# A two-layer decoder step: the odd layer's in-projection and both output projections by seven block products in place of eight, with the sums of weight blocks formed beside the even layer

## The chip, the cores and the metric

The kernel runs on one core of one Trainium2 chip, as one program. The metric is device time in microseconds of that core. The kernel before took 2334.9 us (median of three runs, 2333.31 to 2335.68).

## What is computed

One inference step over a prompt of 2048 tokens and 32 sample rows (8 sequences of 4 tokens), with D = 1024. Each layer normalises its input, projects it, mixes along the tokens, and projects back onto the residual. Cut to the lines that matter here:

```python
def even_mixer(h, w_in, b_fox, lb, hgrn_gain, w_out, hgrn_s0, fox_attend):
    proj = h @ w_in                                       # 1024 -> 4100 columns
    ...                                                   # HGRN2 recurrence on 4 heads, forgetting attention on 4
    out = jnp.concatenate([o_a, o_b], axis=-1) @ w_out    # 1024 -> 1024
def odd_mixer(h, w_in, w_gate, b_gate, gla_gain, w_out, gla_s0):
    proj = h @ w_in                                       # 1024 -> 3088 columns
    q, k, v, g, r = _split(proj, [512, 512, 1024, 1024, 16])
    log_f = jax.nn.log_sigmoid(r @ w_gate + b_gate) / 16
    ...                                                   # gated linear attention on 4 heads, dv = 256
    return o @ w_out, s                                   # 1024 -> 1024
def run_trunk(x, ...):
    for l in range(2):
        x = x + mixer(rmsnorm(x, norm[l]))
    return rmsnorm(x, final_norm), ...
```

## The kernel before, in words

**Products.** Every value that enters a product is scaled by a power of two and kept as two float16 parts, `hi` and `lo`. A product is three matmuls on TensorE (`mm3`): hi x hi, hi x lo, lo x hi. Over 1024 inputs (`KT` = 8 blocks of 128) that makes 24 matmuls for an output tile. They accumulate in a PSUM bank (512 float32 a partition), which VectorE or ScalarE then drains.

```python
    def mm3(self, ps, lh, rh, first, last):
        nc.tensor.matmul(ps, lh[0], rh[0], start=first, stop=False)
        nc.tensor.matmul(ps, lh[0], rh[1], start=False, stop=False)
        return nc.tensor.matmul(ps, lh[1], rh[0], start=False, stop=last)
```

**Units.** A weight unit is 256 columns (272 with the 16 gate columns). `half_unit` gives its four steps: fetch, measure (maximum), scale, and split into hi and lo. The tokens go in two halves of 1024; the 32 samples ride with the first. `proj_tm` puts tokens on the partitions (tiles of 128 tokens x 256 columns, two to a bank), `proj_fm` puts columns there (128 columns x 352 or 512 tokens, banks tagged `pj`, three of them). `few_rows` does the samples as strips of 32 rows, four side by side.

**Stages.** `phase_even` does the even in-projection in two halves of 16 units; the HGRN2 recurrence of a head (`lin_attn`) runs beside the next units. `phase_fox` does attention. `phase_odd` does the even output projection (2 halves x 4 units), the odd in-projection (2 halves x 12 units: for each head values `Cv`, query and key `Cqk`, gate `Cg`) with the recurrences beside it, and the odd output projection (2 halves x 4 units).

**Beside the second even half** `later_unit` reads each of the 20 later weight units once and takes its maximum and scale. The odd stage then fetches each unit again, once for each half, and splits it there.

**Activations.** `y_pieces` splits the mixer's output (`yT`, in memory) into hi and lo for the output projection. Between the layers `norm_store` normalises a tile of 128 rows and writes its hi and lo to `xs` in memory, and `norm_fetch` reads them back transposed, 17 transfers of 512 KB.

**Order.** A generator yields the cost of what it has just issued; `mux` interleaves two of them in proportion. A scheduler then places each instruction in its engine's queue by its own estimate of the times, and each engine takes its queue in order. Weight fetches, stores and transposes are issued by SyncE's queue (SP).

```python
            def recur(hf, h, a):
                return mux(lins[hf](h), LIN_O[hf], dense(a, a + 3), 66000.0)
```

Of the kernel before, what the change touches and what calls it, by code (L numbers as in the profile page):

```python
# [1 line left out]

# [17 lines left out]
P = 128  # L20
D = 1024
# [20 lines left out]
EY = 3  # L42
OY = 2
VPOOL = 1
XO = ("kt", "y", "vp", "c4", "sg")
TAG1 = "o"
PRT = ("st", "o")
# [15 lines left out]
YPOOL = (2, 6)  # L63
# [62 lines left out]
class Kern:  # L126
    def __init__(self, ctx, tc, ins, outs):
        self.ctx, self.tc, self.nc = ctx, tc, tc.nc
        self.i, self.o = ins, outs
        self.loaded, self.bank, self.n_xo = {}, 0, 0  # L130


    def consts(self):
# [30 lines left out]
        self.xs = dp.tile([NTOK, 2 * D], F16, name="xs")  # L164

    def more_consts(self, mp):
# [63 lines left out]
        for g in range(3):  # L230
            m = self.rowmask[g * TS : (g + 1) * TS]
            nc.gpsimd.affine_select(m, m, [[-DS, DB]], ALU.is_ge, 0.0, base=0, channel_multiplier=1)
            nc.gpsimd.affine_select(m, m, [[DS, DB]], ALU.is_ge, 0.0, base=DS - 1, channel_multiplier=-1)

# [87 lines left out]
    def half_unit(self, pool, pps, w, cols, key, nm, undo=None, k=1.0, also=(), raw=("wr", WU), scaler=None):  # L322
# [7 lines left out]
        def fetch():  # L330
            t["raw"] = pool.tile([P, KT, raw[1]], F32, tag=raw[0], name=f"wr_{nm}")
            for a, off, n, src in self.sources(w, cols, h):
                with nc.allow_non_contiguous_dma(reason="a few columns"):
                    nc.sync.dma_start(t["raw"][:, a * h : (a + 1) * h, off : off + n], src)
# [29 lines left out]

    def later_unit(self, pool, pps, w, cols, key, undo=None):

        nc = self.nc
        h, width, t = KT // WSPLIT, sum(n for _, n in cols), {}

        def fetch():  # L370
            t["raw"] = [pool.tile([P, h, WU], F32, tag="lr", name=f"lr_{key}{a}") for a in range(WSPLIT)]
            for a, off, n, src in self.sources(w, cols, h):
                with nc.allow_non_contiguous_dma(reason="a few columns"):
                    nc.sync.dma_start(t["raw"][a][:, :, off : off + n], src)

        def parts():
            t["m"] = pool.tile([P, WSPLIT + 1], F32, tag="rm", name=f"rm_{key}")
            return [r[:, :, :width] for r in t["raw"]]

        return (fetch,) + self.unit_scale(key, parts, lambda: t["m"], pool, pps, key, undo, 1.0)  # L380
# [145 lines left out]
    def norm_store(self, pool, hf, tiles, gain, lead):  # L526
# [3 lines left out]
        todo = self.few_first(self.ttiles(hf))  # L530
        fly = {}

        def load(x):
            c0, n = todo[x]
            fly[x] = [y[:n] for y in tiles(c0)]
            dc = T if c0 >= HALF else hf * HALF + c0
            with ExitStack() as st:
                if self.last_turn is not None:
                    st.enter_context(self.tc.issue_after(self.last_turn.ins))
# [1661 lines left out]
```

## Time and profile before

| What | us |
|---|---|
| median of the runs | 2334.9 |
| span of the profiled execution | 2333.0 |
| even layer, first half | 0 to 478 |
| even layer, second half | 478 to 862 |
| attention | 862 to 1283 |
| even output projection | 1283 to 1452 |
| odd layer, first half | 1452 to 1843 |
| odd layer, second half | 1843 to 2155 |
| odd output projection | 2155 to 2333 |

The borders are where the dense units of a stage begin in the trace; recurrences reach a little over them. In the views a row of a window gives its borders, its length, the busy time of each engine with the number of instructions, then the clock that was granted to TensorE (1.00 is full), the share of the DMA engines and the bandwidth. PE is TensorE's matmuls, PEld its weight loads (which overlap them), DVE VectorE, ACT ScalarE, POOL GpSimd. Matmuls overlap in the records, so that the busy time of one is longer than its share of the pace. A row of the timeline gives start, duration, engine, line, operation and operands (out<-in), and in brackets the idle time ahead of it with what ended it.

### The profile page before, as it was taken

What the parts mean: (1) busy time and instruction counts of PE and PEld (TensorE: products, weight loads), DVE (VectorE), ACT (ScalarE), POOL (GpSimd) and SP (SyncE); (2) the same over time, 40 slices, a digit from 0 to 9 for tenths busy, and PEclk for the clock granted to TensorE, in tenths of its full rate; (3) what the DMA queues carried; (4) which work ended last, traced back from release to release, by engine and by line L of the source; (5) the groups of instructions that cost most, each with busy time, mean ns of one, the idle gap of its engine ahead of it and who ended that gap; (6) DMA issues with size and microseconds to landing.
All of it is one profiled execution on the core that took longest, in us unless ns stands there. A gap on an engine that the chain in (4) does not pass through costs nothing. (4 is left out here: it accounts for less than half of the span.)

```text
span 2333.0 us, 58124 instructions
## 1 busy us (share of the span) xinstructions
PE 2251.4 (96%) x23060; PEld 1603.5 (69%) x23060; DVE 1447.7 (62%) x3313; ACT 1075.0 (46%) x2360; POOL 767.3 (33%) x818
## 2 busy tenths in 40 slices
PE   7999999999999999999999999999999999999998
PEld 5677667864655875665445888677677666666887
DVE  7766568537655757666767445366775655547554
ACT  6434344333332325555656543546545545545343
POOL 2333324112212214223335445144552422322232
PEclk9999999999999999999999999999999999999999
DMA  7232335765441268776982968523233431115553
GB/s 201 66 90 68 96 107 157 179 169 139 145 138 40 90 171 280 230 246 196 275 256 96 337 200 255 147 84 118 75 114 87 122 107 58 46 59 163 161 195 150
DMA packets 375665, 344.87 MB, mean 148 GB/s; under 512 B 107633, under 2 KB 322994, under 8 KB 375394
## 3 DMA queue, kind: packets, MB, share of 16 engines
q1 hardware_dynamic: 373250, 334.54, 48.2%
q0 software_dynamic: 2144, 6.62, 0.8%
q8 instruction: 181, 2.97, 0.5%
q14 instruction: 90, 0.74, 0.1%
HBM read 244.54 MB, written 79.63 MB: 139 GB/s over the span
## 5 line engine op out<-in xcount | busy, mean ns | idle before, releaser
L607 PE MATMUL pt_o<-w_o,act 128*128 128x256 f16 x1024 | 278.7, 273 | 1.8 <-POOL act L1790 1.8
L605 PE MATMUL pt_o<-w_o,act 128*128 128x256 f16 x1024 | 278.9, 273 | 0.6 <-ACT sg1C L662 0.6
L606 PE MATMUL pt_o<-w_o,act 128*128 128x256 f16 x1024 | 278.9, 273 | 0.0
L605 PEld LDWEIGHTS <-act 128*128 128x128 f16 x2304 | 226.6, 98 | 38.0 <-issue 4.0
L607 PEld LDWEIGHTS <-act 128*128 128x128 f16 x2304 | 226.7, 98 | 32.3 <-POOL act L1790 2.2
L606 PEld LDWEIGHTS <-act 128*128 128x128 f16 x2304 | 226.6, 98 | 30.7 <-issue 1.9
L605 PE MATMUL pt_Cv<-w_Cv,act 128*128 128x256 f16 (+1 forms) x512 | 140.9, 275 | 0.1
L606 PE MATMUL pt_Cv<-w_Cv,act 128*128 128x256 f16 (+1 forms) x512 | 141.0, 275 | 0.0
L607 PE MATMUL pt_Cv<-w_Cv,act 128*128 128x256 f16 (+1 forms) x512 | 140.9, 275 | 0.0
L772 POOL TENSOR_TENSOR kA<-kA,fA 128x512 f32<-128x512 f32 (+1 forms) x56 | 78.0, 1392 | 188.6 <-PE gl_A L738 142.5
L772 POOL TENSOR_TENSOR kC<-kC,fC 128x512 f32<-128x512 f32 (+1 forms) x56 | 83.6, 1492 | 153.4 <-PE gl_C L738 101.7
L1407 POOL TENSOR_SCALAR L<-L,nm 128x512 f32<-128x512 f32 (+3 forms) x160 | 99.3, 635 | 98.2 <-DVE nm L1403 42.3
L1399 ACT ACTIVATE L<-L,nm,kc 128x512 f32<-128x512 f32 (+3 forms) x160 | 118.3, 741 | 24.7 <-DVE nm L1397 23.8
L1434 ACT ACTIVATE th<-pt 128x512 f16<-128x512 f32 (+3 forms) x159 | 81.8, 528 | 90.2 <-PE pt L1427 87.0
L1435 DVE TENSOR_TENSOR tl<-pt,th 128x512 f16<-128x512 f32 (+3 forms) x159 | 95.2, 609 | 20.5 <-ACT th L1434 18.6
L1427 PE MATMUL pt<-ident,L 128*128 128x128 f32 x544 | 90.3, 278 | 1.4 <-POOL L L1407 1.0
L1551 PEld LDWEIGHTS pkt<-ident,pgcache_fox_k 128*128 128x128 f32 x512 | 58.4, 141 | 43.3 <-issue 25.1
L1889 ACT ACTIVATE vC<-pt_Cv,kc 128x512 f32<-128x512 f32 (+1 forms) x40 | 23.9, 598 | 129.8 <-PE pt_Cv L607 129.8
L1427 PEld LDWEIGHTS pt<-ident,L 128*128 128x128 f32 x544 | 66.5, 143 | 24.6 <-DVE tl L1435 4.8
L1551 PE MATMUL pkt<-ident,pgcache_fox_k 128*128 128x128 f32 x512 | 77.6, 278 | 5.5 <-DVE kts L1556 1.6
L1374 POOL TENSOR_TENSOR cm<-cb,caus 128x128 f32<-128x128 f32 x64 | 29.0, 454 | 135.7 <-DVE mx L1391 114.5
L605 PE MATMUL pt_Bk<-w_Bk,act 128*128 128x256 f16 x256 | 71.4, 279 | 2.3 <-DVE Bvs L1049 2.3
(959 smaller groups left out, 6752.9 us busy)
## 6 DMA issues: line engine op xcount, KB each, us to landing
pgcache_fox_k<-in_cache_fox_k SPq DMA_DIRECT2D x128, 256.0 KB, 4.2
pgcache_fox_v<-in_cache_fox_v SPq DMA_DIRECT2D x128, 256.0 KB, 4.1
yr<-yT SPq DMA_DIRECT2D x16, 1024.0 KB, 7.9
x1d<-xo SPq DMA_DIRECT2D x44, 256.0 KB, 4.2
wr_Aqf<-in_w_in_even SPq DMA_DIRECT2D x64, 128.0 KB, 3.3
wr_o<-in_w_out_even SPq DMA_DIRECT2D x32, 256.0 KB, 5.2
xo<-in_x_prompt SPq DMA_DIRECT2D x32, 256.0 KB, 5.2
wr_Cv<-in_w_in_odd SPq DMA_DIRECT2D x32, 256.0 KB, 4.0
```

The costliest lines, as they stand in the source:

```text
L605: nc.tensor.matmul(ps, lh[0], rh[0], start=first, stop=False)
L606: nc.tensor.matmul(ps, lh[0], rh[1], start=False, stop=False)
L607: return nc.tensor.matmul(ps, lh[1], rh[0], start=False, stop=last)
L772: nc.gpsimd.tensor_tensor(kv[:, :, 0], kv[:, :, 0], t1.to_broadcast([P, nb, w]), ALU.mult)
L1374: self.last_cm = nc.gpsimd.tensor_tensor(cm, cb[:, tb * P : (tb + 1) * P], caus, ALU.add)
L1399: self.last_exp = nc.scalar.activation(lt[:, :w], lt[:, :w], AF.Exp, bias=nm[:, 0:1], scale=ib, accum_out=nm[:, 2 + j : 3 + j])
L1407: nc.gpsimd.tensor_scalar(lt[:, :w], lt[:, :w], nm[:, 1:2], 2.0**14, ALU.mult, ALU.mult)
L1427: nc.tensor.transpose(pt[:, w : w + P], rows[b][s // 4][0][:, (s % 4) * P : (s % 4 + 1) * P], self.ident)
L1434: nc.scalar.activation(th[:, a:w], pt[:, a:w], AF.Copy),
L1435: nc.vector.tensor_tensor(tl[:, a:w], pt[:, a:w], th[:, a:w], ALU.subtract)))
L1551: last = nc.tensor.transpose(pk[:, j * P : (j + 1) * P], pgs[j][:, h * P : (h + 1) * P], self.ident)
L1889: r = nc.scalar.activation(v[h][:, g : g + cnt], ps[:, :, :256], AF.Copy, scale=c)
```

## The change

With the tokens of a half (or of a piece) as two row blocks, the 1024 inputs as two column blocks, and the columns of a unit as two blocks, a product of 2 x 2 blocks takes eight block products. The change takes seven (one level of the Strassen-Winograd form). The seven left operands are A11, S1, S2, S4, S3, A12, A22, where S are sums and differences of blocks of activations, and the right ones B11, T1, T2, B22, T3, B21, T4 of weights. The output's sums are made by accumulation: three banks, x, z and y, take the products in the order x z x z x y x, and a bank is drained after each product, with add, into the output block that needs it at that point.

```diff
+SEVEN = (("x", "A11", "B11"), ("z", "S1", "T1"), ("x", "S2", "T2"), ("z", "S4", "B22"), ("x", "S3", "T3"),
+         ("y", "A12", "B21"), ("x", "A22", "T4"))
+INTO = ((0, 0), (1, 1), (0, 1), (0, 1), (1, 1), (0, 0), (1, 0))
+SIDE0 = 3
+AHEAD = 400
...
+    def seven(self, pps, mm, ev, nm):
+        self.n7 += 1
+        tags = {b: f"p{(self.n7 + x) % 3}" for x, b in enumerate("xzy")}
...
+        for s, (bank, a, b) in enumerate(SEVEN):
...
+                ps[bank] = pps.tile([P, 512], F32, tag=tags[bank], name=f"ps{bank}_{nm}")
+            mm(ps[bank], a, b, first)
+            with self.tc.high_priority(AHEAD):
+                ev(s, ps[bank])
+            yield 2600
```

**Weights.** `later_unit` goes. From the fourth unit of the first even half on (`SIDE0` = 3), `side_work` reads the 20 later units, measures them, forms their seven right operands each (sums on GpSimd, hi on ScalarE, lo on VectorE) and stores them in memory (`wc`, 140 pieces of 256 KB; the gate columns in `wr`). The odd stage loads them as they are; fetch, measure, scale and split leave it.

```diff
-    def later_unit(self, pool, pps, w, cols, key, undo=None):
...
+    def side_unit(self, pool, pps, w, cols, key, u, mx=None, last=True, known=False):
...
+        def split(o, x):
+            s = self.scales[key][:, 0:1]
+            nc.scalar.activation(o[:, 0], x, AF.Copy, scale=s)
+            nc.vector.scalar_tensor_tensor(o[:, 1], x, s, o[:, 0], ALU.mult, ALU.subtract)
+
+        def part(name, x):
+            o = pool.tile([P, 2, 4, P], F16, tag="tw", name=f"tw{u}{name}")
+            split(o, x)
+            nc.sync.dma_start(self.wc[u][:, RIGHT.index(name)], o)
...
+        def two():
+            nc.gpsimd.tensor_tensor(b(0, 1), b(0, 1), b(0, 0), ALU.subtract)
+            part("T3", b(1, 1))
+            nc.gpsimd.tensor_tensor(b(0, 0), b(0, 0), b(1, 1), ALU.add)
```

**Output projections.** Each is eight pieces of 256 tokens (two tiles of 128 rows). `y_parts` scales a piece and forms its seven left operands. `piece` multiplies them with right operands of all 1024 columns that stay in SBUF. In the even one each of three bank tags has two buffers; after a piece of the first half, `norm_pair` normalises its two row tiles, forms their seven sums, stores them in `xs`, and `left_fetch` reads them back transposed (28 transfers of 256 KB). The rows of the second half are normalised beside the first odd half and fetched in 7 transfers of 1 MB.

```diff
+    def left_sums(self, a11, a12, a21, a22, part):
+        part("A11", a11, nc.vector)
+        nc.gpsimd.tensor_tensor(a11, a11, a21, ALU.subtract)
+        part("A22", a22, nc.gpsimd)
+        nc.gpsimd.tensor_tensor(a21, a21, a22, ALU.add)
+        part("S1", a21, nc.vector)
+        nc.gpsimd.tensor_tensor(a22, a22, a11, ALU.subtract)
+        part("S2", a22, nc.vector)
+        part("A12", a12, nc.vector)
+        nc.gpsimd.tensor_tensor(a12, a12, a22, ALU.subtract)
+        part("S4", a12, nc.vector)
+        part("S3", a11, nc.gpsimd)
...
+    def piece(self, pps, A, B, rows, c, done, nm):
+            for k in range(4):
+                self.mm3(v, [A[a][:, x, k] for x in range(2)], [B[b][:, :, x, k] for x in range(2)],
+                         first and k == 0, k == 3, True)
+        def ev(s, t):
+            g, half = INTO[s]
+            d = rows[g][:, half * 512 : half * 512 + 512]
+            nc.vector.scalar_tensor_tensor(d, t, c, d, ALU.mult, ALU.add)
...
+            pps = Pool(stage.enter_context(pool("ops", space=PSUM)), {"p0": 2, "p1": 2, "p2": 2, "f": 2})
```

**Odd in-projection.** The 12 units of a half each go through `seven`. Query, key and gate products are 128 columns of weights by 512 tokens; a value product is 4 tiles of 128 tokens by 128 columns. The first drain of an output block is ScalarE's copy, the second VectorE's add from the bank. The gate columns go as strips, folded by a small matmul (`gates_r`), in place of transposes. Each bank tag has one buffer here and in the odd output projection.

```diff
-            pps = Pool(None, {"pj": 3, "gr": 2, "st": 1, "o": 2})
+            pps = Pool(late.enter_context(pool("gps", space=PSUM)), {"p0": 1, "p1": 1, "p2": 1, "gr": 2, "st": 1, "o": 2})
...
+            def ev(s, ps):
+                t, x = INTO[s]
+                d, e = into(t, x)
...
+                if (t, x) not in got:
+                    got.add((t, x))
+                    nc.scalar.activation(d, src, AF.Copy, scale=e)
...
+                else:
+                    nc.vector.scalar_tensor_tensor(d, src, e, d, ALU.mult, ALU.add)
...
+                return mux(lins[hf](h), LIN_O[hf], dense(a, a + 3), 54600.0)
```

**What stands in the queues.** VectorE, second even half, third head's recurrence. Names: `qA`, `fA` and `scT` are the recurrence's, `rm` and `pow` a later unit's maximum and scale, `tw12B` and the like an operand of later unit 12, L1299 its lo part. Before:

```order
L753 COPY_PREDICATED scT_868<-mlev_822,gl_A_8829 30x8x8x2 x4
L771 TENSOR_TENSOR qA_8501<-qA_8501,fA_8502 128x256x2
L773 TENSOR_TENSOR fA_8502<-fA_8502 128x256
L288 TENSOR_REDUCE pow_o_9059<-spr_o_9057 128x1
L299 TENSOR_REDUCE rm_o_9325<-lr_o_9213 128x1
```

Now:

```order
L770 COPY_PREDICATED scT_878<-mlev_825,gl_A_8106 30x8x8x2 x4
L788 TENSOR_TENSOR qA_7289<-qA_7289,fA_7290 128x256x2
L1299 SCALAR_TENSOR_TENSOR tw12B_8720<-lr_o_8019,kc,tw12B_8720 128x512
L790 TENSOR_TENSOR fA_7290<-fA_7290 128x256
L1299 SCALAR_TENSOR_TENSOR tw12T_8724<-lr_o_8016,kc,tw12T_8724 128x512
L1299 SCALAR_TENSOR_TENSOR tw12T_8767<-lr_o_8019,kc,tw12T_8767 128x512
L770 COPY_PREDICATED scT_878<-mlev_831,gl_A_8203 28x8x4x4 x4
```

Three lo parts of 512 elements now stand between two steps of the recurrence, where a reduction of a maximum stood.

GpSimd, even output projection. Names: `raw` is a piece's activations, `row` a residual tile, `xo` and `y0` left operands, `grow` the next norm's gain. Before:

```order
L1790 TENSOR_TENSOR act<-yr_20309,act 128x2x256 x2
L1790 TENSOR_TENSOR act<-yr_20321,act 128x2x256 x2
L360 TENSOR_TENSOR w_o_20501<-wr_o_20079,w_o_20501 128x2x256 x2
L548 TENSOR_TENSOR x1r_20333<-x1r_20333,grow 32x1024
L412 TENSOR_TENSOR rsr_n_20520<-rst_n_20518,mhalf 32x1
```

Now:

```order
L535 TENSOR_TENSOR row_19712<-row_19712,grow 128x1024
L410 TENSOR_TENSOR rsr_n<-rst_n,mhalf 128x1
L564 TENSOR_TENSOR raw_20124<-raw_20124,raw_20125 128x512
L554 TENSOR_TENSOR row_19711<-row_19711,row_19712 128x512
L545 TENSOR_TENSOR xoA_20225<-row_19712,xoA_20225 128x512
L1901 TENSOR_TENSOR y0S_20474<-raw_20124,y0S_20474 128x512
L557 TENSOR_TENSOR row_19712<-row_19712 128x512
L1901 TENSOR_TENSOR y0A_20549<-raw_20308,y0A_20549 128x512
L554 TENSOR_TENSOR raw_20307<-raw_20307,raw_20308 128x512
```

The sums of a piece's activations and those of a norm's rows now stand in one queue, in turn.

VectorE, odd first half, beside the first head's recurrence. Names: `psz`, `psx` and `psy` are the banks, `kC` and `qC_22806` the next head's key and query. Before:

```order
L771 TENSOR_TENSOR qC_22687<-qC_22687,fC_22919 128x264x2
L773 TENSOR_TENSOR fC_22919<-fC_22919 128x264
L786 COPY kr_C_23608<-kC_22688 128x96
L789 TENSOR_TENSOR hl_C_23607<-ktS_C_23606,hl_C_23607 32x128
L800 TENSOR_TENSOR kpad_C_23616<-hl_C_23607,rowmask 96x512
```

Now:

```order
L2117 SCALAR_TENSOR_TENSOR kC_22807<-psz_C_22916,kc,kC_22807 128x512
L788 TENSOR_TENSOR qC_21636<-qC_21636,fC_21505 128x8x64
L738 SCALAR_TENSOR_TENSOR y_C00S_22932<-py_C00S_22930,g_gla,sg0C_21814 128x16 x2
L790 TENSOR_TENSOR fC_21505<-fC_21505 128x8
L861 TENSOR_TENSOR pd_C00s_22959<-scT_877,pd_C00s_22959 128x256
L2117 SCALAR_TENSOR_TENSOR kC_22807<-psx_C_22809,kc,kC_22807 128x512
L738 SCALAR_TENSOR_TENSOR y_C00S_22938<-py_C00S_22936,g_gla,sg1C_21815 128x16 x2
L861 TENSOR_TENSOR kt_C00k_22950<-kt_C_22947,kt_C00k_22950 128x256
```

Drains of a bank (L2117) now stand among the recurrence's steps in VectorE's queue. Before, ScalarE alone drained query and key.

903 lines of the change are left out of this document (527 added, 376 removed).

## The prediction

> **What bounds the kernel now.** The page comes first: its span and TensorE's busy time.
>
> ```profile
> span 2333.0 us, 58124 instructions
> PE 2251.4 (96%) x23060; PEld 1603.5 (69%) x23060; DVE 1447.7 (62%) x3313; ACT 1075.0 (46%) x2360; POOL 767.3 (33%) x818
> ```
>
> TensorE is busy 96% of the span, no other engine more than 69%. So fewer TensorE columns are worth their time, as long as TensorE isn't made to wait. The busy time by stage, the second view, tells where it would be made to wait. In it stand even layer first half and two stretches of it, even second half, even output projection, odd first half, odd second half, odd output projection.
>
> ```profile
> core 0: us, PE busy (x) PEld busy (x) DVE busy (x) ACT busy (x) POOL busy (x), PEclk, DMA share, GB/s
> 84.00:478.00 394.00, 382.96 (x4589) 288.78 (x4587) 255.36 (x566) 153.66 (x359) 122.06 (x95) 0.99 0.40 112
> 155.00:238.00 83.00, 82.75 (x1052) 62.95 (x1051) 53.26 (x121) 34.44 (x91) 28.39 (x22) 1.00 0.29 88
> 352.00:420.00 68.00, 62.97 (x847) 52.84 (x845) 54.45 (x130) 31.06 (x76) 27.18 (x23) 0.97 0.56 169
> 478.00:862.00 384.00, 380.27 (x4028) 247.62 (x4026) 228.78 (x528) 127.26 (x291) 83.25 (x74) 1.00 0.42 121
> 1283.00:1452.00 169.00, 167.19 (x1592) 147.45 (x1590) 85.56 (x104) 79.48 (x131) 83.69 (x58) 1.00 0.84 264
> 1452.00:1843.00 391.00, 379.29 (x4437) 279.69 (x4435) 239.35 (x481) 195.22 (x410) 157.16 (x122) 0.99 0.42 113
> 1843.00:2155.00 312.00, 307.36 (x3332) 206.56 (x3330) 177.89 (x345) 159.71 (x335) 87.54 (x78) 1.00 0.27 83
> 2155.00:2333.00 178.00, 168.70 (x1793) 148.90 (x1791) 95.89 (x192) 67.09 (x174) 54.00 (x63) 0.99 0.50 167
> ```
>
> In each, TensorE's busy time is within 5% of the stage, at a granted clock of 0.99 or 1.00. The exception is the stretch 352 to 420: VectorE is busy 54.45 of 68 us (80%) there, and TensorE idles 5.0 us (7.4%). At 64% VectorE (155 to 238) it idled 0.25 of 83 us. A busy matmul is no measure of columns, since records overlap, so the pace is read from starts in the timeline.
>
> ```profile
> 1399.78 0.27 PE L606 MATMUL pt_o<-w_o,act 128*128 128x256 f16 x1
> ...
> 1402.95 0.27 PE L605 MATMUL pt_o<-w_o,act 128*128 128x256 f16 x1
> ```
> ```profile
> 1482.74 0.31 PE L606 MATMUL pf_C00q<-act,w_Cqk 128*128 128x352 f16 x1
> ...
> 1485.87 0.31 PE L606 MATMUL pf_C00q<-act,w_Cqk 128*128 128x352 f16 x1
> ```
> ```profile
> 1845.30 0.38 PE L606 MATMUL pf_C10k<-act,w_Cqk 128*128 128x512 f16 x1
> ...
> 1849.40 0.38 PE L607 MATMUL pf_C10k<-act,w_Cqk 128*128 128x512 f16 x1
> ```
> ```profile
> 862.32 0.22 PE L605 MATMUL s<-k,q 128*128 128x128 f16 x1
> 862.37 0.22 PE L606 MATMUL s<-k,q 128*128 128x128 f16 x1
> 862.43 0.22 PE L607 MATMUL s<-k,q 128*128 128x128 f16 x1
> ```
>
> Between the first pair lie 29 steps: 109.3 ns for 256 columns. The second has 21 steps, 149 ns for 352; the third 19, 215.8 ns for 512. For 128 columns it is 55 to 56 ns, and each of those had a weight load of its own. Pace follows columns, down to 128.
>
> **The change: the products.** Before: 16 half units of output projection, 8 tiles of 24 matmuls each, 3072 x 109.3 ns = 335.8 us. The values (Cv) take 1536, of which 384 have 272 columns (by the same pace 116 ns): 170.5 us. Query, key and gate take 1152 of 352 columns (171.6) in the first half, 768 of 512 (165.7) in the second. Together 843.6 us. After: 16 pieces and 16 query-key and gate units of 7 x 12 matmuls with 512 columns, 2688 x 215.8 = 580.1 us, and 8 value units of 7 x 48 with 128 columns, 2688 x 56 = 150.5 us: 730.6 us. That takes **113.0 us** off.
>
> Some comes back with the 32 sample rows and the gate columns, which run as strips, four side by side.
>
> ```profile
> 1299.12 0.40 PE L650 MATMUL pS_o<-w_o,sam_o 128*32 128x256 f16 x6
> 1299.99 0.51 PE L650 MATMUL pS_o<-w_o,sam_o 128*32 128x256 f16 x11
> 1300.75 0.40 PE L650 MATMUL pS_o<-w_o,sam_o 128*32 128x256 f16 x7
> ```
>
> Those 24 strips took at most 1.31 us, 55 ns each; a quarter of 109.3 is 27. The program has 720 new strips of 128 columns, 120 of 512 and 96 of 512 for the gate (202,752 columns), and drops 288 of 256 (73,728). The difference, 504 strips' worth, is 13.6 to 27.7 us: +20. Twenty-five small folding products against 17 transposes gone are put at +2 (0 to 8). Net: **-91 us** (-99 to -77).
>
> **The side work in the even layer.** Twenty weight units are each split into seven operands: 140 ScalarE copies, 140 VectorE subtracts, 80 GpSimd sums and 140 stores. Maxima were taken there before too. Prices come from the groups, and from the per-line view (least/median/longest, ns):
>
> ```profile
> L352 ACT ACTIVATE w_o<-wr_o,kc 128x512 f16<-128x512 f32 x32 | 22.6, 707 | 0.0
> L353 DVE SCALAR_TENSOR_TENSOR w_o<-wr_o,kc,w_o x32: 730/1093/2505, 1267.4 to 2264.3; 128x512 f16<-128x512 f32 x32
> L771 DVE TENSOR_TENSOR qA<-qA,fA x56: 676/693/1641, 108.1 to 797.6; 128x512 f32<-128x512 f32 x48, 128x528 f32<-128x528 f32 x8
> L772 POOL TENSOR_TENSOR kA<-kA,fA x56: 1053/1374/2407, 105.3 to 796.2; 128x512 f32<-128x512 f32 x48, 128x528 f32<-128x528 f32 x8
> L360 POOL TENSOR_TENSOR w_o<-wr_o,w_o x32: 1146/1231/2288, 1275.5 to 2263.8; 128x512 f16<-128x512 f32 x32
> L548 POOL TENSOR_TENSOR x1r<-x1r,grow x17: 2347/2361/3332, 1390.2 to 1716.9; 128x1024 f32<-128x1024 f32 x16, 32x1024 f32<-32x1024 f32 x1
> L1836 DVE SCALAR_TENSOR_TENSOR xo<-pt_o,kc,xo x48: 732/750/753, 1298.1 to 2246.2; 128x512 f32<-128x512 f32 x48
> ```
>
> ScalarE gains 140 x 0.707 = 99 us, GpSimd 80 x 1.374 = 110, VectorE 140 x 0.730 to 1.093 = 102 to 153. From 84 to 862 us VectorE was busy 255.4 + 228.8 of 778 us, 62%; now it is 75 to 82%. Nothing waits for this work before the out projection, but VectorE runs in order, and the recurrence's own steps stand behind it. At worst the whole 778 us idles as 352 to 420 did: 0.074 x 778 = 58, less the 14.8 idle there now: +43. At best it fills idle time: 0. I take the middle, **+22**, because the row at 64% lost nearly nothing and the one at 80% is the nearest to the new share. The weight work that leaves the later stages (per half unit 6 copies, 2 VectorE and 2 GpSimd operations) only relieves engines that were not the bound, so I count nothing for it.
>
> **The out projections' operands.** Each piece of 256 tokens needs four GpSimd sums and two GpSimd subtracts (4 x 1.053 + 2 x 1.146 = 6.5 us) and five VectorE subtracts (3.4), beside 84 x 215.8 ns = 18.1 us of products: covered. In the even projection four norms are added, each 2.35 + 6.5 on GpSimd and 1.5 (1024 elements, twice 0.730) + 3.4 on VectorE. GpSimd has 8 x 6.5 + 4 x 8.9 = 88 us of 145: covered, if the norms spread over the stage. DMA stood at 0.84 at 264 GB/s for 169 us (44.6 MB); now activations, rows and their store (8.4 MB each), sums and transposes (7.3 each) and the first weights (about 3) make some 43 MB in 151 us, so near full. **+6** (0 to 21, derived below).
>
> **The single banks.** In the odd stage and its out projection a product's bank is drained before the product after next, which accumulates in it: 24 x 7 + 8 x 7 = 224 drains with one product (12 x 215.8 ns = 2.59 us) as cover. Before, three banks of 24 matmuls went round.
>
> ```profile
> 1334.28 0.27 PE L607 MATMUL pt_o<-w_o,act 128*128 128x256 f16 x1
> ...
> 1334.59 0.75 DVE L1836 SCALAR_TENSOR_TENSOR xo<-pt_o,kc,xo 128x512 f32<-128x512 f32 x1 [0.64 <-PE pt_o L607]
> ```
>
> A drain that finds VectorE free is done at 1335.34, 0.95 us after the last matmul's columns (1334.28 + 0.11). That leaves 1.6 us for what stands ahead in VectorE's or ScalarE's queue, two operations of 0.7 us. With VectorE at 61% (239 of 391) and 57% most fit. I take 0.05 us a drain, **+12**; nothing at best, and what it could be at worst is the last rival.
>
> **Sum.** 2333.0 - 91 + 22 + 6 + 12 = 2282 us of span. The runs' median, 2334.9, is 1.9 us above this span: **2284 us**. The tail after the last product (normalising a row tile, storing it) keeps its kind; I count no change.
>
> **Rivals.** *Everything hidden*: the side work falls into idle slots as the weight work did, and 2334.9 - 91 = 2244. For it: 14.8 us idle in 778 now. Against it: the 80% stretch.
>
> *A lock between VectorE and GpSimd.* A VectorE operation with two SBUF inputs runs 730 ns at least, 1093 in the middle and 2505 at worst (L353), while one that reads a bank and one SBUF tile never leaves 732 to 753 (L1836). GpSimd's subtract, too, doubles at worst (1146 to 2288). So such pairs seem to take turns. The change adds to both sides. Where a norm runs beside a piece, the two-input work is 6.5 + 3.4 + 8.9 + 4.9 = 23.7 us against 18.1 of products; if each norm stays with one piece that is 4 x 5.6 = 22 us, 21 with rounding, and the even layer loses its full 43: 2334.9 - 91 + 43 + 21 + 12 = 2320. Against it: spread over eight pieces it is 8 x 9.9 + 4 x 13.8 = 134 of 145 us. The Trainium skill, page "SBUF — State Buffer", section "Who interferes with whom", says just this: two SBUF inputs on VectorE and a GpSimd operation that reads SBUF exclude each other for a whole instruction. The two rows above agree with it; by that rule alone the time would be this rival's.
>
> *Slower: the banks.* If drains start late as a rule, every product of the odd stage waits. The price is 224 times the mean wait beyond the cover. With 22 and 6 lost elsewhere it takes (91 - 28) / 224 = 0.28 us a drain to be slower than before, that is, a drain standing 1.9 us in its queue. At 0.35 us: 2334.9 - 91 + 28 + 78 = 2350. For it: in-order queues shared with the recurrence, one bank where there were three. Against it: VectorE free 39% of the time, and recurrence products between the block products.
>
> **Chances.** Forecast 0.45 (2262 to 2305 is its own range), all hidden 0.24, lock 0.19, banks 0.12. The range 2240 to 2340 leaves out most of the last and a small part of the second, under 2 in 10. Runs of this kernel spread 0.1%, so 0.2% is about what a measurement can tell. Faster 0.86, within 0.2% 0.03, slower 0.11: a sliver of the lock's and banks' cases falls near 2335.
>
> **What would show it.** TensorE's matmul count and pace give the 113 (products of 512 columns 216 ns apart, of 128 columns 56). TensorE's idle from 84 to 862 above 15 us is the side work's price, and its VectorE share should be 75 to 82%. In the odd stage the waits of products for drains add up to about 12 us. In the even projection idle ended by GpSimd or DMA is under 21. I am wrong if 128-column products run slower than 56 ns, if the transposes hold up a half's first unit, or if the drains' waits exceed 60 us.

## The result, and the profile after

The changed kernel takes 2426.74 us (median of four runs, 2424.22 to 2428.83), the kernel before 2334.11 in the same job: a ratio of 1.0396, 95% interval 1.0382 to 1.0411. It is 92 us slower; 2284 was forecast, in a range of 2240 to 2340.

The page after: span and busy time of each engine.

```profile
span 2422.5 us, 57934 instructions
PE 2222.1 (92%) x22601; PEld 1412.4 (58%) x22601; DVE 1641.3 (68%) x3364; ACT 1107.4 (46%) x2372; POOL 927.0 (38%) x919
```

TensorE's busy time fell by 29 us, the span grew by 89.5. So TensorE waits: 200 us of its span, where it was 82. The busy time by stage shows where. The rows are even layer first half, even second half, attention, even output projection, odd in-projection, odd output projection.

```profile
0.00:382.50 382.50, 345.48 (x3731) 243.83 (x3732) 302.56 (x643) 171.79 (x380) 140.16 (x142) 0.96 0.52 152
382.50:937.50 555.00, 512.90 (x5391) 352.06 (x5390) 392.85 (x694) 248.29 (x516) 217.37 (x164) 0.97 0.55 168
937.50:1365.30 427.80, 396.00 (x2785) 233.81 (x2784) 299.95 (x919) 245.17 (x560) 152.80 (x271) 0.98 0.75 233
1365.30:1536.30 171.00, 155.32 (x737) 68.01 (x735) 116.03 (x136) 76.14 (x118) 113.05 (x81) 0.98 0.86 251
1536.30:2192.10 655.80, 619.60 (x8616) 416.68 (x8615) 373.19 (x711) 268.12 (x577) 192.70 (x165) 0.98 0.45 129
2192.10:2422.50 230.40, 192.81 (x1353) 98.05 (x1351) 156.75 (x262) 97.91 (x223) 110.95 (x98) 0.95 0.38 126
```

The same rows of the kernel before, cut at its own borders:

```profile
0.00:351.60 351.60, 332.96 (x3715) 237.05 (x3716) 232.30 (x542) 153.65 (x351) 108.93 (x121) 1.00 0.36 104
351.60:862.30 510.70, 501.55 (x5419) 351.15 (x5418) 314.57 (x716) 176.03 (x402) 118.57 (x104) 0.99 0.48 135
862.30:1282.90 420.60, 394.23 (x2785) 232.63 (x2784) 302.19 (x935) 243.83 (x559) 157.39 (x273) 0.98 0.73 225
1282.90:1456.70 173.80, 171.99 (x1637) 151.76 (x1634) 85.93 (x104) 79.48 (x131) 84.42 (x59) 1.00 0.85 264
1456.70:2131.00 674.30, 660.56 (x7360) 463.42 (x7358) 395.46 (x787) 343.07 (x722) 238.15 (x195) 0.99 0.33 94
2131.00:2333.00 202.00, 190.09 (x2157) 167.52 (x2155) 117.29 (x230) 78.96 (x196) 59.82 (x67) 0.99 0.53 175
```

Three parts can be read from each row: the length less TensorE's busy time is its idle time; the length times one less the granted clock is what the slower clock lost (the table uses the clock with more digits); the rest is work at full clock. The table sets them side by side, in us.

| Stage | before: length, idle, clock | after: length, idle, clock | change of work, idle, clock |
|---|---|---|---|
| even layer | 862.3, 27.8, 5.1 | 937.5, 79.1, 30.7 | -1.7, +51.3, +25.6 |
| attention | 420.6, 26.4, 6.8 | 427.8, 31.8, 8.5 | +0.1, +5.4, +1.7 |
| even output projection | 173.8, 1.8, 0 | 171.0, 15.7, 3.4 | -20.1, +13.9, +3.4 |
| odd in-projection | 674.3, 13.7, 3.4 | 655.8, 36.2, 13.7 | -51.2, +22.5, +10.2 |
| odd output projection | 202.0, 11.9, 2.5 | 230.4, 37.6, 12.5 | -7.3, +25.7, +10.0 |
| sum | 2333.0, 81.6, 17.8 | 2422.5, 200.4, 68.8 | -80.2, +118.8, +51.0 |

(At the borders the recurrences of one stage reach into the next, so the last two rows are best read together.) The work fell by 80 us, most of it the products; the forecast had -99 to -77. Idle time took 119 and the clock 51. The split isn't sharp: some of the half clock fell on time in which TensorE stood anyway (8.6 us of the 68.8, before 3.1 of 17.8), and without that the clock took 45 and the work fell by 75.

How the two hang together is seen at one place of the even layer. Rows of short windows: TensorE busy, then standing, then working again, then later.

```profile
197.40:201.20 3.80, 3.80 (x42) 3.05 (x32) 3.80 (x6) 1.37 (x4) 3.80 (x3) 1.00 0.19 69
201.40:205.30 3.90, 0.01 (x1) 0.00 (x0) 3.77 (x9) 1.29 (x3) 0.67 (x1) 1.00 0.52 149
206.30:209.60 3.30, 3.30 (x17) 2.29 (x16) 3.18 (x8) 0.00 (x0) 1.99 (x2) 0.50 1.05 346
209.70:213.00 3.30, 3.30 (x91) 2.43 (x90) 1.56 (x4) 0.84 (x2) 0.79 (x2) 1.00 0.63 214
```

TensorE stands 3.9 us, and then runs at half clock for a stretch of 3.41 us. The trace after has 30 such stretches (3.41, 6.83 or 10.24 us long, the last cut off by the end); 26 of them have a wait of 1.8 us or more in the 6.8 us ahead of them. Before there were ten. The timeline of VectorE, GpSimd and TensorE tells what the wait was for.

```profile
200.17 0.51 DVE L681 SCALAR_TENSOR_TENSOR Bg<-th_B,Bg 128x352 f32<-128x352 f32 x1
200.60 1.54 DVE L1319 TENSOR_TENSOR lr_Cv<-lr_Cv,lr_Cv 128x64 f32<-128x64 f32 x1
202.08 0.51 DVE L681 SCALAR_TENSOR_TENSOR Bg<-th_B,Bg 128x352 f32<-128x352 f32 x1
202.51 1.82 DVE L770 COPY_PREDICATED scT<-mlev,gl_A 31x128 f32<-31x128 int8 x4
204.36 0.29 DVE L781 COPY_PREDICATED scTs<-mlev,gls_A 32x64 f32<-32x64 int8 x1
204.50 0.69 DVE L788 TENSOR_TENSOR qA<-qA,fA 128x528 f32<-128x528 f32 x1
```
```profile
200.13 1.95 POOL L789 TENSOR_TENSOR kA<-kA,fA 128x528 f32<-128x528 f32 x1
```
```profile
205.34 0.69 PE L755 MATMUL gl_A<-qA,kA 128*30 128x16 f32 x62 [3.93 <-DVE qA L788]
```

VectorE was busy 3.77 of those 3.90 us. A subtraction of 64 elements of the side work (L1319) took 1.54 us and ended at 202.14, with GpSimd's step of the recurrence (kA, a multiplication), which ended at 202.08. Behind it in VectorE's queue stood the recurrence's step (L788) for which TensorE waited 3.93 us. That is the prediction's lock, its in-order queue, and a price that it left out: the clock.

### The profile page after: what moved, and what is told of

The parts are those of the page before. It is cut to its first block, busy times and chain, and to the rows that moved or that the text cites. A ratio compares the mean times of both kernels' runs of the same rounds, so it can differ in the third digit from the quotient of the medians.

```text
span 2422.5 us, 57934 instructions
## 1 busy us (share of the span) xinstructions
PE 2222.1 (92%) x22601; PEld 1412.4 (58%) x22601; DVE 1641.3 (68%) x3364; ACT 1107.4 (46%) x2372; POOL 927.0 (38%) x919
## 5 line engine op out<-in xcount | busy, mean ns | idle before, releaser
L1549 ACT ACTIVATE th<-pt 128x512 f16<-128x512 f32 (+3 forms) x159 | 81.9, 529 | 97.2 <-PE pt L1542 91.7
L622 PEld LDWEIGHTS <-act 128*128 128x128 f16 x768 | 77.0, 100 | 13.7 <-DVE Bks L1066 1.5
L623 PEld LDWEIGHTS <-act 128*128 128x128 f16 x768 | 76.9, 100 | 13.0 <-issue 2.0
L624 PEld LDWEIGHTS <-act 128*128 128x128 f16 x768 | 76.9, 100 | 11.3 <-issue 0.9
L1542 PEld LDWEIGHTS pt<-ident,L 128*128 128x128 f32 x544 | 66.5, 143 | 26.4 <-DVE tl L1550 5.9
L622 PE MATMUL pt_Av<-w_Ai,act 128*128 128x256 f16 x256 | 73.3, 286 | 0.4 <-DVE Bvs L1066 0.4
L623 PE MATMUL pt_Av<-w_Ai,act 128*128 128x256 f16 x256 | 73.2, 286 | 0.4 <-DVE w_Ai L368 0.4
L624 PE MATMUL pt_Av<-w_Ai,act 128*128 128x256 f16 x256 | 73.4, 287 | 0.0
L622 PE MATMUL pt_Bv<-w_Bv,act 128*128 128x260 f16 (+1 forms) x256 | 70.6, 276 | 2.4 <-DVE Bvs L1066 1.8
L788 DVE TENSOR_TENSOR qC<-qC,fC 128x512 f32<-128x512 f32 (+1 forms) x56 | 51.4, 917 | 31.4 <-PE gl_C L755 30.5
L622 PE MATMUL pt_Bk<-w_Bk,act 128*128 128x256 f16 x256 | 70.7, 276 | 0.5 <-DVE Bks L1066 0.5
L623 PE MATMUL pt_Bk<-w_Bk,act 128*128 128x256 f16 x256 | 70.8, 277 | 0.0
L624 PE MATMUL pt_Bv<-w_Bv,act 128*128 128x260 f16 (+1 forms) x256 | 70.7, 276 | 0.0
```

The source lines that it names most:

```text
L622: nc.tensor.matmul(ps, lh[0], rh[0], start=first, stop=False, skip_group_check=grows)
L623: nc.tensor.matmul(ps, lh[0], rh[1], start=False, stop=False, skip_group_check=grows)
L788: nc.vector.tensor_tensor(xv[:, :, 1], xv[:, :, 1], t0.to_broadcast([P, nb, w]), ALU.mult)
L1542: nc.tensor.transpose(pt[:, w : w + P], rows[b][s // 4][0][:, (s % 4) * P : (s % 4 + 1) * P], self.ident)
L1549: nc.scalar.activation(th[:, a:w], pt[:, a:w], AF.Copy),
```

## The experiments

Unless it says "the kernel before", an edit is one of the changed kernel (2426.7 us, first attention score at 937.5). A time is the median of two runs. The kernel before took 2329.8 to 2334.8 in these jobs.

### What the even layer pays for, by taking parts away

**e1, lo on GpSimd** (ScalarE scales a weight block in place first)

```diff
-            nc.vector.scalar_tensor_tensor(o[:, 1], x, s, o[:, 0], ALU.mult, ALU.subtract)
+            nc.gpsimd.tensor_tensor(o[:, 1], x, o[:, 0], ALU.subtract)
```

> The side work's 140 lo parts go from VectorE to GpSimd (ScalarE first scales each weight block in place; 40 more ScalarE operations). Theory A (VectorE's in-order queue delays the recurrences, and TensorE idles and then runs at half clock): from 0 to the first attention score VectorE's busy share falls from about 80% to about 65%, TensorE's idle time there from 79 us to under 45, the clock's loss from 31 us to under 15, and the time from 2426.7 to 2360-2385. Theory B (VectorE and GpSimd exclude each other, the sum of both counts): GpSimd gains 160 us, so no gain: 2415-2450.

2442.5 us; first score at 949.9, 12 us later. The second even half, busy time by stage:

```profile
378.00:949.90 571.90, 514.63 (x5393) 355.58 (x5391) 322.47 (x580) 266.50 (x541) 337.85 (x271) 0.96 0.53 163
```

VectorE is down to 322 of 572 us (56%, less than the 62% before the change), and TensorE idles 57 us there, where it was 42. Theory A, VectorE's share, fell. Of the 57, 20.5 now wait for GpSimd's own step of the recurrence (kA), 28 for VectorE.

**e2, lo as a second ScalarE copy** (the subtraction is left out)

```diff
-            nc.vector.scalar_tensor_tensor(o[:, 1], x, s, o[:, 0], ALU.mult, ALU.subtract)
+            nc.scalar.activation(o[:, 1], x, AF.Copy, scale=s)
```

> The side work's 140 subtractions are left out (lo is a second scaled copy by ScalarE), so VectorE loses 140 operations and GpSimd gains none. Theory A: as in the run with lo on GpSimd, 2360-2385, even layer about 50 us shorter. Theory B: VectorE's operations no longer meet GpSimd's 80 sums as often, a gain too, but lo on GpSimd must then be at least 30 us slower than this one. Theory C (the even layer's loss comes from the 36.7 MB of stores and the extra reads): no change, 2415-2435.

2407.0, first score at 917.3: 20 us earlier, less than half of what A asked, and 35 us faster than e1, as B asked. C fell. From 84 us to the first score VectorE's share is 61% here and 62% in e1, as in the kernel before; yet the layer is 55 and 88 us longer than there.

**e3, no sums of weights** (operands are plain blocks: the four `nc.gpsimd.tensor_tensor` lines of steps `one` to `four` are left out)

> The 80 GpSimd sums of weight blocks are left out (operands are plain blocks). Theory A: VectorE keeps its 140 lo parts, so the even layer stays within 15 us of 937 and the time is 2410-2428. Theory B: GpSimd loses 125 of its 338 us in the even layer, VectorE's two-input operations get shorter, and the even layer wins 30 us or more: under 2400.

2409.0, first score at 921.9: between the two. The lo parts became shorter (mean 0.93 to 0.84 us).

**e16, sums on VectorE** (in the same four lines `nc.vector` for `nc.gpsimd`)

> The side work's 80 sums go from GpSimd to VectorE (0.69 us each where GpSimd takes 1.5). By the lock, VectorE gains 55 us of work and wins back some 40 us of stretched operations: even layer within 10 us of 937, or up to 20 shorter as GpSimd's own steps of the recurrence come earlier; time 2405-2435. By VectorE's share alone: 15 to 30 us longer, 2440-2457.

2427.7, first score at 936.6: nothing. The lo parts fell to 0.80 us, VectorE's busy time in the layer rose from 695 to 707. What VectorE takes over, it gets back from GpSimd.

**e6, a fourth buffer** (`ETW = 4`)

> Four buffers for formed operands in place of three. ScalarE stood 54 us ahead of side instructions for a load or a store's landing. If these waits for buffers block the recurrences behind them: even layer 8 to 25 us shorter (912-930), time 2402-2419. If VectorE's share alone counts: no change, 2420-2432.

2428.3: nothing. Waits for these buffers aren't what blocks.

**e5 and e11, no forming at all** (operands are constants, and the second reading of the output weights is left out too; the stores stay, seven for a unit in e5, one in e11)

```diff
-        return fetch, [measure, scale, one, two, three, four, five]
+        return fetch, [measure, lambda: (scale(), fill())]
```

> Of the side work only the maxima and scales stay; the operands are not formed, and a constant tile is stored in their place (all 140 stores, 36.7 MB, but no second reading of the output weights). If the forming of operands (its chain of load, GpSimd sum, ScalarE hi, VectorE lo, store, through four in-order queues) is the price: first attention score at 862-875 instead of 937, idle plus clock loss ahead of it under 45 us instead of 110, time 2350-2365. If the stores or the scheduler's new order are: first score after 900, time over 2385.

> The changed kernel without the forming of operands, as in the run of that kind before, but each unit's seven constant tiles are stored by one transfer in place of seven (that run's stores stood in a row of 30 in SP's queue for 21.6 us, and the store of qd behind them held up ScalarE 20.9 us and TensorE 12.7). If the row of stores was a cost of that run alone: first score at 875-890 instead of 898. If reading and measuring in both halves costs by itself: it stays at 893-900.

e5: 2395.9, first score at 898.5, 39 us earlier. It isn't a clean zero: 30 stores stood in a row in SyncE's queue, 21.6 us long, and a store behind them held up TensorE 12.7 us. e11 was worse, 2450.6: 11 stores of 1.8 MB stood in a row in SyncE's queue, 47.5 us long, and behind them the loads of a weight unit, for whose maximum TensorE waited 51.4 us in one piece. It tells only that a row of large stores delays the loads behind it. How far the layer falls without forming is so bounded on one side: by 39 us or more, of 75.

### What it pays for, by adding parts to the kernel before

**e9 and e10**: the kernel before with 140 VectorE operations of the lo form, and (e10) 140 ScalarE copies and 80 GpSimd sums too, none depending on another. They read a tile that 56 small loads fill.

```diff
+                        if e == "v":
+                            nc.vector.scalar_tensor_tensor(dl, dr, 2.0, dl, ALU.mult, ALU.subtract)
+                        elif e == "a":
+                            nc.scalar.activation(dh, dr, AF.Copy, scale=2.0)
+                        else:
+                            nc.gpsimd.tensor_tensor(dg, dg, dr, ALU.add)
```

> The kernel before, with 140 VectorE operations of the lo parts' form added in the even layer, spread as the side work is. Each waits for nothing but a 256 KB load of its own (56 loads), and nothing waits for it. If VectorE's share alone is the price (the prediction's view): first attention score 20 to 45 us later than 862, time 2355-2380. If the chain through four queues is the price, operations that are ready when their turn comes cost little: score within 10 us of 862, time 2333-2345.

> As the run before, with 140 ScalarE copies and 80 GpSimd sums added as well, each independent of the others: the side work's operations without its chain. Chain theory: still under 15 us, 2335-2350. Share and lock (VectorE and GpSimd stretch each other): 40 to 75 us, 2375-2410, and VectorE's two-input operations grow as in the changed kernel (qA from 864 to about 918 ns).

2390.1 and 2464.2; first score at 918.6 and 987.1, 56 and 125 us later than before. Independent work costs more than the change's own chain did (75). The added VectorE operation by the per-line view (least/median/longest, ns), e9 first:

```profile
L1140 DVE SCALAR_TENSOR_TENSOR dl<-dr,dl x140: 669/691/2725, 85.1 to 792.0; 128x512 f16<-128x512 f32 x140
...
  DMA dr<-in_x_prompt: 84.7, 23
```
```profile
L1140 DVE SCALAR_TENSOR_TENSOR dl<-dr,dl x140: 670/919/2572, 84.0 to 858.8; 128x512 f16<-128x512 f32 x140
...
  DMA dr<-in_x_prompt: 85.8, 23
```

The mean goes from 781 to 1128 ns (busy 109.4 and 158.0 us over 140). VectorE stood as long ahead of these operations for their loads in both (85 us), so the second 69 us aren't waits of VectorE for loads. But the added operations of the other engines wait for the same loads, GpSimd's sums by far the longest, and ScalarE's copies 79.8 us:

```profile
L1144 POOL TENSOR_TENSOR dg<-dg,dr x80: 1257/1602/3703, 84.1 to 853.9; 128x512 f32<-128x512 f32 x80
...
  DMA dr<-in_x_prompt: 176.9, 28
```

GpSimd's waits don't reach TensorE. From 84 us to the first score, e9 against e10, TensorE's waits for GpSimd are 5.9 and 5.2 us, VectorE's for GpSimd 10.3 and 9.8. ScalarE's may in part: TensorE's waits for ScalarE grow from 1.9 to 13.5 us, those for VectorE from 43.8 to 81.9.

**e13 and e14**: the same operations, reading weights that have been loaded for the next units (`dr` is `self.seen[:, 2:4, :256]`, the raw tile measured or split last; no loads of their own).

> The kernel before with 140 VectorE operations of the lo parts' form, as in the run with loads of their own, but they read weights that VectorE has measured already, so none waits for a load (those 140 stood 85 us ahead of their loads in VectorE's queue). If the waits at the head of the queue are the price: first attention score under 877 (15 us later than before), time under 2352. If VectorE's work itself is: 895-915, 2365-2390, nearly as with the loads (918.6, 2390).

> As the run before with 140 ScalarE copies and 80 GpSimd sums of the same weights added, none of which waits for a load or for another engine's new work. Queue-wait theory: first score under 890, time under 2365. Work and lock: the added lo-form operations take about 1100 ns (781 without the sums), and the first score comes 80 us later or more, time over 2410.

2362.0 and 2428.8; first score at 895.3 and 954.4, 33 and 92 us later.

```profile
L1136 DVE SCALAR_TENSOR_TENSOR dl<-wr_Aqf,dl x30: 672/692/1972, 124.4 to 596.6; 128x512 f16<-128x512 f32 x30
```
```profile
L1136 DVE SCALAR_TENSOR_TENSOR dl<-wr_Aqf,dl x30: 672/1586/1867, 130.9 to 638.6; 128x512 f16<-128x512 f32 x30
```

For the 30 that read one of the tiles the median goes from 692 to 1586 ns; over all 140 the mean goes from 0.77 to 1.20 us. The trace of e14 tells which engine stretches them: the 34 that no GpSimd instruction overlapped took 693 ns at most, beside ScalarE or not; the other 106 took 1.36 us in the mean, and the 75 over 1 us all ended 0.545 to 0.554 us after a GpSimd instruction did, as if they stood until it was done. (In the changed kernel 68 of the 140 lo parts had no GpSimd beside them and took 753 ns at most; 34 took over 1 us, and they too ended 0.545 to 0.553 us after a GpSimd instruction.)

The queue-wait theory had asked for under 15 and under 28 us, and missed by far. But these kernels didn't take all waits away: some operations were queued ahead of the measuring they were meant to follow, and VectorE still stood 72 and 69 us ahead of them for weights; in e14 GpSimd stood 107 us and ScalarE 39. TensorE's and VectorE's waits for GpSimd didn't grow (5.7 to 4.8, 13.9 to 12.0 us), TensorE's for ScalarE grew by 6.5, for VectorE by 34. VectorE's own waits didn't grow either, but up to the first score it was busy 714.6 us where it was 640.8, for the same 1397 instructions. So most of the 59 us between the two is VectorE's lateness, by operations stretched beside GpSimd; the small part through ScalarE isn't told apart, and of the first 33 a part may be waits.

### The output projections

**e7, single banks in the even projection** (`{"p0": 1, "p1": 1, "p2": 1, "f": 2}`)

> The even output projection with one buffer for each bank tag in place of two: 56 drains with one product as cover. By the prediction's price (0.05 us a drain) the stage grows by 3 us, within noise of 2427; by the price of the rival (0.28 to 0.35 us) by 16 to 20 us, to 2443-2447. The idle time of that stage, ended by VectorE's drains, was 15.7 us with two.

2439.8. The stage takes 181.7 us, 10.8 more; over 56 drains that is 0.19 us each, idle time and clock together, between the prediction's 0.05 and the rival's 0.28. (It is the price against two buffers, and in this stage, not in the odd ones.)

**e8, no sums of activations** (the four `nc.gpsimd` lines of `left_sums` are left out)

> The GpSimd sums of activation blocks are left out (4 for each piece and each pair of normalised row tiles, 96 in all; the hi and lo parts stay). If GpSimd's sums stretch VectorE's lo parts (mean 1178 ns where 680 is the least) and so make the drains late: lo parts fall to 700-850 ns, idle in the even output projection from 15.7 to under 7 us, odd output projection 5-15 us shorter, time 2400-2415. If VectorE's own load or the recurrences set the waits: within 6 us of 2427.

2417.8, 9 us less, between the two forecasts: 3.6 us in the even projection and 4.6 in the odd one. In the even projection the idle time stayed at 14.6 us, and the lo parts of a piece on VectorE fell only from 1.09 to 0.92 us in the mean, so the condition of the first forecast wasn't met. GpSimd's sums are a small part of that idle time.

**e4, four pieces beside the last recurrence**

```diff
-            drain(mux(lins[1](3), LIN3_B, last(0, 2), 36400.0))
-            drain(last(2, 8))
+            drain(mux(lins[1](3), LIN3_B, last(0, 4, 4), 72800.0))
...
+            drain(last(4, 8))
```

> Four pieces of the odd output projection in place of two are spread beside the last recurrence; the other four follow it. If the last recurrence leaves TensorE without work (29 us idle and half clock from 2192 on), the stretch from the first product of this projection to the end falls from 230 us to 200-215 and the time to 2395-2415. If the single banks' drains are the cause, the waits only move: 2420-2435.

2426.7 (two runs far apart, 2419.0 and 2434.4), and 231.4 us for the stage where it was 230.5: nothing. The changed kernel's own rows show where this stage loses: four windows beside the last recurrence, and one after it.

```profile
2192.10:2230.00 37.90, 34.00 (x185) 20.98 (x183) 21.99 (x48) 13.47 (x43) 8.73 (x11) 1.00 0.48 165
2230.00:2260.00 30.00, 20.39 (x381) 9.81 (x382) 24.83 (x41) 9.29 (x13) 17.86 (x14) 0.83 0.39 116
2260.00:2290.00 30.00, 24.73 (x208) 11.58 (x207) 20.11 (x28) 11.81 (x26) 18.41 (x14) 0.89 0.00 1
2290.00:2326.00 36.00, 28.38 (x199) 17.88 (x197) 25.27 (x55) 22.88 (x59) 19.43 (x20) 1.00 0.58 190
2326.00:2414.00 88.00, 85.31 (x384) 37.79 (x383) 62.08 (x88) 38.30 (x79) 45.73 (x40) 0.98 0.38 131
```

From 2326 on, with products alone, TensorE idles 2.7 of 88 us. From 2230 to 2260 VectorE is busy 83% (drains, final norms, lo parts and the recurrence), TensorE idles 9.6 of 30 us and has 0.83 of its clock.

### The odd in-projection

**e15, without the second drains** (the `else:` branch with VectorE's add in `ev` is left out)

> The changed kernel without the 72 VectorE additions that drain a bank a second time in the odd in-projection (the first drains, by ScalarE, stay). If late drains of single banks set the odd stage's loss, it falls by 20-35 us with its half clock, time 2390-2407. If the recurrences and transfers do: by less than 12 us, 2415-2427.

2425.4: nothing, though VectorE's share in the stage fell from 57 to 48%. So VectorE's load there isn't the cause. The banks aren't cleared by it: of the 9.4 us that the products of the changed kernel's odd in-projection waited for drains, 8.1 were ended by ScalarE's first drains, which stay, and only 1.3 by these additions.

**e12, transposes in quarters** (`for j in range(4): self.left_fetch(self.A, 1, j, 1)`)

> The second odd half's activations are fetched in 28 transfers of 256 KB, tile by tile, in place of 7 of 1 MB. Idle ended by these transfers was 6.4 us, with 10 to 17 us at half clock behind it. If their size is the cause, products of whole tokens blocks still wait for all four quarters, so the last to land decides: a gain of at most 3 us or a loss; if the order of operands is: 5 to 12 us less, 2415-2422.

2427.1: nothing; the size of the transfers isn't it.

**e18, without the second half's fetch** (`self.left_tiles(apool, 1)` and `left_fetch` left out)

> The changed kernel without the transposing fetch of the second odd half's activations (the second half multiplies the first half's again). The seven 1 MB transfers overwrite the buffers that the last unit of the first half reads, so they can't start early; idle ended by them was 6.4 us, and 17 us of half clock lie within 60 us behind the border. If the border is a main cost of the odd stage: 10 to 18 us less, 2409-2417. If not: 2420-2430.

2404.9: 22 us, more than expected. The odd in-projection and output projection, as a whole:

```profile
1538.20:2174.20 636.00, 613.27 (x8615) 414.98 (x8614) 373.01 (x711) 268.81 (x577) 193.33 (x165) 0.99 0.41 122
2174.20:2404.50 230.30, 194.19 (x1353) 98.48 (x1351) 157.52 (x262) 97.83 (x223) 110.44 (x98) 0.94 0.38 127
```

Against the changed kernel's 655.8 that is 20 us in the in-projection: 13.5 of idle, 8.5 of clock, the work within 2. It lies at the border between the halves: in the 120 us from 20 us ahead of the second half's first product, idle time falls from 17.6 to 2.9 us and the clock's loss from 10.3 to nothing.

**e17, six products in place of seven**

```diff
             def mm(ps, a, b, first):
+                if a == "S4":
+                    return
```

> The changed kernel without one of the seven block products (S4 by B22) in the 24 units of the odd in-projection; all drains stay. That takes 24 x 2.6 = 62 us of TensorE's columns from the stages beside the odd recurrences. If TensorE's columns still bound these stages, the time falls by 50 to 62 us, to 2365-2377. If the recurrences' chain over VectorE, ScalarE and GpSimd has become the bound (each has now less block product beside it), idle and half clock fill what is freed and the time falls by 10 to 30 us only, to 2397-2417.

2388.5: 38 us less, between the two forecasts.

```profile
1537.40:2156.90 619.50, 565.55 (x7992) 383.10 (x7991) 364.88 (x708) 265.06 (x570) 192.74 (x163) 0.96 0.47 138
```

The in-projection is 36 us shorter than 655.8, while TensorE's idle grew from 36 to 54 us and the clock from 0.98 to 0.96. Of 62 us of columns about 60% show in the time. The rest goes to waits: of 18 us more idle time, 9 lie ahead of the small matmuls of the recurrences and gates, 5 wait for transfers, 4 for drains and other work ahead of the products.

## Why the prediction was wrong

**The products: right, at the edge of the range.** -91 was forecast, -80 came (-75 by the stricter count of the clock). Products of 512 columns run 2.59 us for 12, as forecast, and the pace of 128 columns held.

**The side work: mis-sized, +22 for +75.** The step that failed is "I take the middle". The price of the row at 80% (7.4% idle) came in full: from 84 to 937.5 TensorE idled 65 of 853.5 us, 7.6%. That is +50 (+51 from 0 on) where the stated worst was 43, and it came at a VectorE share of 74%, under the row's 80%. The other 26 are the clock. The same row had it, 0.97, and the prediction read that number and counted only the idle time. At 3% of 778 us it would have been 23 more. And the share, by which the prediction chose between its two rows, is no measure of the price: e1 and e2 have the share of the kernel before and lost 88 and 55 us. What counts is when VectorE comes to the recurrence's step: of the 65 us, 56.5 were ended by VectorE (before, 10.9 of 14.8).

The lock, a rival at 0.19, is the mechanism that the runs bear out best. Work without any chain between its parts, added to the kernel before, costs 92 to 125 us (e14, e10); GpSimd's sums and ScalarE's copies add 59 to 69 to what VectorE's part costs alone, and VectorE's operation grows by half, by GpSimd alone (e14). Moving work across the lock gains nothing (e16) or loses (e1). The Trainium skill, page "SBUF — State Buffer", section "Who interferes with whom", has this rule, and these runs agree: a 64-element subtraction takes 1.54 us until GpSimd's multiplication ends. The rival's own price, 2320, was too low: for the even layer by the clock and a cap at 43, and it had the same +12 for the odd stages. What part late loads have in it isn't settled: they, too, hold up a queue that is taken in order.

**The even output projection: +6 for +17** (13.9 idle, 3.4 clock), within its range of 0 to 21. All its waits were for VectorE's drains, none for GpSimd or DMA; "covered" compared sums over the stage, and a drain waits for what stands ahead of it at that moment.

**The odd stages: +12 for +68.** They lost 48 us to idle and 20 to the clock, and the sum had one term for them, the drains of single banks. Some of TensorE's longest waits there (us, times, longest):

```profile
PE psx_C L622 <- ACT vC L2113: 3.8, 2, 2.0
PE gl_C L755 <- DVE qC L788: 3.8, 3, 2.3
PE psz_C L622 <- DMA a1S<-xs: 3.5, 2, 1.9
```
```profile
PE psx_o L622 <- DVE rw L1965: 8.6, 6, 5.0
PE gl_C L755 <- DVE qC L709: 4.3, 1, 4.3
```

All together, the products waited 21 us for drains (9.4 in the in-projection, 11.6 in the output projection), where 12 was forecast: "most fit" was too hopeful, and e7's 0.19 us a drain says the same of another stage. The larger part has no term in the sum. Matmuls of the recurrences and gates waited 31 us (before, all waits of these stages came to 17). Transfers were waited for 8 us, 6.6 of them for the transposes of the second half's activations, and with the other waits around that border and the clock it is 22 (e18); the prediction named "if the transposes hold up a half's first unit" as a sign of being wrong and gave it no price. Operands of the output projection took 4. Columns taken away from the in-projection return 60% (e17): the sentence "fewer TensorE columns are worth their time, as long as TensorE isn't made to wait" had the condition, and the sum didn't price it. The rival with the banks asked for 78 us by drains alone; the trace has 21. No run changed the banks of the odd stages, so what they cost in time is read from the waits only.

**The clock: left out, +51**, and counted above in each stage. **Attention: nothing was forecast, +7.** No run tells why.

What stays open: how the even layer's 75 us divide between forming, reading and waits for loads (39 or more go with forming and the second reading of the output weights), what part of the lock's 59 to 69 us comes by ScalarE, and what the odd stages' banks cost in time. No run that computes the whole step came under 2334 us with the change in it.

## What to carry to other kernels

Where one engine is busy 96%, price a saving on it by what its cover gives back: work beside a chain of small steps may return only a part of its time (60% here, e17). Work moved to "idle" engines is to be priced by the row that shows the worst stretch, taken in full, idle time and granted clock together; the share of the engine that takes it says too little. And where VectorE's operations with two SBUF inputs run beside GpSimd's, don't price them at their time alone (0.69 us; beside GpSimd 1.36 in e14).

## What the runs showed of the hardware

A wait of TensorE can cost more than itself: 119 us more of idle time brought 51 us of lost clock with it. All 30 stretches of half clock in the trace after start on one grid of 3.413 us, to within 4 ns. In the grid's step ahead of each, TensorE stood for 1.75 us or more in sum. Of the steps at full clock, 37 had so much idle time, and 30 of them were followed by half clock; of 627 with less, none was. (Before, 8 of the 10 stretches follow such a step, in e17 31 of 36.) So short waits add up (a stretch at 28.73 has no wait over 1.2 us ahead of it, but 1.86 us in sum), and a wait that is shared by two steps may cost only itself (2.34 us, ended at 1807.86). This grid is read from these traces; no run was made to test it. The Trainium skill, page "TensorE: Matmul & The Clock Gate", section "What's actually happening", has the two states and a window of about 3.4 us, and the trace's stretches agree. Its section "HAM oscillation — how this bites in real kernels" gives as the rule no idle gaps over about 3.4 us; here waits of 1.8 to 2.5 us are followed by half clock too (a wait of 2.37 us that ended at 136.34 by a stretch of 10.24 us).

Where VectorE's lo operation of 128x512 (0.69 to 0.75 us alone) took over 1 us, it ended 0.545 to 0.554 us after a GpSimd instruction, in all 75 cases of e14, 69 of e10 and 34 of the changed kernel. That reads as standing until GpSimd's instruction ends, and not as a slower pace beside it.
